# A new plan for the attention steps, and a last layer norm in four pieces, in a one-core decoder block

## The chip, the cores and the metric

The kernel runs on one core of a Trainium2 chip. The metric is device time in microseconds, from the start to the end of one execution. The kernel before has a median of 1132.72 us over 3 runs (1132.64 to 1136.57).

## The reference, cut to what matters

One decoder layer over 256 tokens of width 1024, all in float32. The mixer makes one projection of `x` and runs two attentions on its columns: sliding-window attention with a learned sink per head, and a three-branch sparse attention. The MoE part sends each token to 4 of 32 experts.

```python
h = LayerNorm(alpha * x + Mixer(x))
y = LayerNorm(alpha * h + MoE(h))
# mixer A, per head; mixer B's branches are the same without the sink
s = q @ k.T * scale + bias            # masked to the window
m = max(max(s), sink)
e = exp(s - m)
p = e / (sum(e) + exp(sink - m))
o = p @ v
# MoE, for each expert with its tokens
act = glu * sigmoid(1.702 * glu) * (lin + 1)
out = act @ w_down[e] + b_down[e]
```

## The kernel before, in words

**Three stages.** First comes the mixer. TensorE (PE) runs 32 projection units. A unit is one block of 128 columns: a weight of 8 blocks of 128x128 is multiplied with the 256 tokens, three times, since weights and tokens are split into a high and a low part. So a unit has 24 matmuls and falls into two halves of 12. The halves are numbered h; half h belongs to unit h/2, rounded down. After the units come the branch projections, the output projection, the first layer norm and the router. The second stage is the 32 experts, whose weights (12 MB each) are streamed from memory through ten fixed buffers: a transfer can only start when the buffer's last content has been used up. The third stage is the last layer norm (`finish`) with the output's four transfers.

**How attention is laid between the units.** The 12 head pairs (branch b = 0, 1, 2 and pair r = 0 to 3) each take four steps. S (`scores`, L605): PE makes the scores, VectorE (DVE) adds the bias and takes the row maximum, ScalarE (ACT) takes the exponential and its sum. N (`norm`): DVE inverts the sum, GpSimd (POOL) multiplies four pieces by it. T (`transpose`): six PE transposes into two PSUM tiles, each copied to SBUF as `pT`. V (`pv`): eight matmuls, and the result is taken out of PSUM. So `S10` is the S step of branch 1, pair 0. `PLAN` (L48) says after which half each step is called. `vt` transposes v, `bias1` loads the second bias table into the buffer of the first, `bl` and `bs` load and split the expert biases, `mlp`, `gelu`, `ckv` compute the compressed blocks (tiles `phid`, `phidT`, `pkc`), `ct` and `cp` use them, `sig` takes the sigmoids of the merge gates (tile M).

**What sets the order.** The orders of PE and of the DMA-issuing SyncE queue (SP) are as the program calls them. In the mixer the orders of DVE, ACT and POOL are set by a scheduler when the program is built; after that, every engine works through its own list in order, and an instruction that must wait holds up all that stands behind it. Around the experts and in `finish` all orders are written out.

**Splitting weights.** `prep` calls `split_w` two units ahead: the high part is a rounding copy (on ACT, or on POOL where `POOL_PART` has 'h'), the low part a subtraction (on DVE, or on POOL where it has 'l'). Three buffers `w_j` take turns, so the rounding for unit n must wait until PE has finished unit n-3.

**PSUM tiles that take turns.** The transposes, `pvt`, `phid`, `phidT`, `pct` share two buffers (tag `t`); a step that takes a buffer waits until the tile two places earlier has been copied out. The lines on which the steps rest:

```python
ps_t = ctx.enter_context(tc.tile_pool(name="ps_t", bufs=2, space=PSUM))
ps_s = mx.enter_context(tc.tile_pool(name="ps_s", bufs=3, space=PSUM))
SP.dma_start(T[b], src)             # load_T: both tables in one buffer of tag "T"
```

Of the kernel before, what the change touches and what calls it, by code (L numbers as in the profile page):

```python
# [47 lines left out]
PLAN = {7: 'gates', 8: 'sinks', 9: 'c1', 10: 'gsum S00 S02', 11: 'S01 N00 N01', 12: 'N02', 13: 'T00 S03 N03 bias1 T02', 14: 'vt0 V00 T01', 15: 'V01 blocks', 16: 'V02 T03', 17: 'V03 mlp bl', 19: 'gelu', 20: 'bs', 22: 'bw', 23: 'ckv S10 N10', 24: 'S11 N11 br', 26: 'S12 T10 N12', 27: 'T11 S13 N13', 28: 'vt1 csm', 29: 'T12 V11 S20', 30: 'V10 T13 N20', 31: 'ct V13 vt2', 32: 'S21 V12 T20 cp1 cp0 S22 N22 V20 S23', 33: 'N21 T21 N23', 34: 'cp2 cp3 V21 T22', 35: 'rw V22 T23', 36: 'x V23', 38: 'sel', 39: 'sig'}  # L48
# [11 lines left out]
def tile_block(ctx: ExitStack, tc: tile.TileContext, a, out):  # L60
# [541 lines left out]
    class Pair:  # L602
# [3 lines left out]
        def scores(self):  # L606
# [54 lines left out]

        def transpose(self):
            self.pT = []
            for g in range(2):
# [445 lines left out]
    class Expert:  # L1110
# [3 lines left out]
        def gate_up(self, j):  # L1114
# [91 lines left out]
    def finish():  # L1206
        lo, mid, hi = slice(0, 512), slice(512, SPLIT), slice(SPLIT, D)
        (st0, ag0, rs0), (st1, ag1, rs1) = lns
        g_, b_ = ln2[:, 0], ln2[:, 1]

        def normed(tt, rs):
            o_ = oz[:, tt]
            ACT.activation(o_[:, 512:], yac[tt][1], AF.Identity, bias=rs[:, 0:1], scale=rs[:, 1:2])
            POOL.tensor_tensor(o_[:, hi], o_[:, hi], g_[:, hi], ALU.mult)
            POOL.tensor_tensor(o_[:, hi], o_[:, hi], b_[:, hi], ALU.add)

        def rest(tt):
            o_ = oz[:, tt]
            DVE.tensor_tensor(o_[:, mid], o_[:, mid], g_[:, mid], ALU.mult)
            DVE.tensor_tensor(o_[:, mid], o_[:, mid], b_[:, mid], ALU.add)  # L1220

        for o_ in range(2):
            DVE.bn_stats(st0[:, o_, :], yac[0][o_])
        ln_scale(st0, ag0, rs0)
        for o_ in range(2):
            DVE.bn_stats(st1[:, o_, :], yac[1][o_])
        ln_inv(ag0, rs0)
        normed(0, rs0)
        ln_scale(st1, ag1, rs1)
        ln_mean(oz[:, 0], yac[0][0], g_, lo, ag0)  # L1230
        ln_inv(ag1, rs1)
        normed(1, rs1)
        ln_dev(oz[:, 0], b_, lo, rs0)
        rest(0)
        ln_mean(oz[:, 1], yac[1][0], g_, lo, ag1)
        ln_dev(oz[:, 1], b_, lo, rs1)
# [169 lines left out]
```

## Time and profile before

| | us |
|---|---|
| median of 3 runs | 1132.72 |
| the profiled execution | 1130.43 |
| its span, first to last instruction | 1128.7 |
| mixer, until the first expert's matmuls | 206.7 |
| DVE's first statistics of the last norm | 1114.15 |

PE is busy in 95% of the span, DVE in 26%, ACT in 18%, POOL in 7%. The 16 DMA engines move 438.5 MB, at about 427 GB/s in most slices of the span. A busy PE is not PE at its peak, since the ends of its pipelined matmuls are modelled; the starts of successive instructions tell more. Of a row of the timeline, the first number is the start in us, the second the duration, and the bracket, where there is one, the idle time of that engine before it and what released it.

### The profile page before, as it was taken

The numbers are of one execution on the slowest core, as the hardware profiler recorded it, in microseconds if no ns is written. First come the engines' busy times: TensorE is split into PE (matmuls) and PEld (weight loads), VectorE is DVE, ScalarE is ACT, GpSimd is POOL, SyncE is SP. The second block draws the span as 40 slices with busy tenths as digits, with TensorE's granted clock in tenths as the row PEclk, the third lists the DMA queues.
The fourth block names the chain that finished last, engine by engine and source line by source line (L and its number), as shares of the span: only waits on it lengthen the run. The fifth ranks groups of instructions, "written<-read, shape, count | busy, mean of one in ns | idle before, by whom it ended". The sixth has DMA issues, their size and how long they took to land.

```text
span 1128.7 us, 13459 instructions
## 1 busy us (share of the span) xinstructions
PE 1069.2 (95%) x5660; PEld 509.7 (45%) x5660; DVE 290.0 (26%) x710; ACT 203.8 (18%) x434; POOL 79.4 (7%) x115
## 2 busy tenths in 40 slices
PE   9899999999999999999999999989999998899895
PEld 8787998543434343334343333333333342333322
DVE  4887366311111111111121211111110211020213
ACT  3545344210101110111110101011111110011011
POOL 1545310000000000000000000000000000000001
PEclk9999999999999999999999999999998999999998
DMA  9583777899999999999999999999999999999993
GB/s 335 195 310 137 305 298 299 333 403 418 426 427 426 428 429 427 427 428 426 428 427 427 426 426 427 427 430 427 426 427 427 426 429 427 427 426 427 426 427 123
DMA packets 38288, 438.50 MB, mean 389 GB/s; under 512 B 4032, under 2 KB 6736, under 8 KB 9168
## 3 DMA queue, kind: packets, MB, share of 16 engines
q1 hardware_dynamic: 37888, 436.98, 92.7%
q8 instruction: 46, 0.75, 0.3%
q10 hardware_dynamic: 336, 0.62, 0.2%
q14 instruction: 18, 0.15, 0.0%
HBM read 435.92 MB, written 1.66 MB: 388 GB/s over the span
## 4 chain that ended last, share of the span: by engine, by line


## 5 line engine op out<-in xcount | busy, mean ns | idle before, releaser
L1123 PE MATMUL g<-wg,xeM 128*64 128x512 f32 x1208 | 282.2, 605 | 2.3 <-DMA wg<-in_w_gu_dram 2.2
L1123 PEld LDWEIGHTS g<-wg,xeM 128*64 128x64 f32 x1208 | 83.4, 138 | 157.0 <-issue 140.2
L1145 PE MATMUL pd<-wd,wk 128*64 128x512 f32 x600 | 134.1, 594 | 15.4 <-DMA wd<-in_w_d_dram 15.4
L1123 PE MATMUL g<-wb,xeM 128*64 128x512 f32 x624 | 145.2, 600 | 1.5 <-DMA wb<-in_w_gu_dram 1.5
L1150 DVE COPY y<-pd 64x512 f32<-64x512 f32 x32 | 22.2, 694 | 426.7 <-ACT y L1149 426.7
L1145 PEld LDWEIGHTS pd<-wd,wk 128*64 128x64 f32 x600 | 42.9, 137 | 101.3 <-issue 81.0
L1103 DVE TENSOR_SCALAR gs<-g 128x512 f32<-128x512 f32 x32 | 22.1, 692 | 247.2 <-PE g L1123 247.2
L1123 PEld LDWEIGHTS g<-wb,xeM 128*64 128x64 f32 x624 | 42.9, 138 | 83.2 <-issue 73.9
L1145 PE MATMUL pd<-wb,wk 128*64 128x512 f32 x304 | 69.8, 606 | 7.0 <-DMA wb<-in_w_d_dram 7.0
L1149 ACT COPY y<-pd 64x512 f32<-64x512 f32 x32 | 18.5, 578 | 293.9 <-PE pd L1145 293.9
L247 PE MATMUL pu<-xhl,w_j 128*128 128x256 f32 x240 | 70.1, 292 | 0.0
L1037 POOL TENSOR_SCALAR wk<-const,posm 128x64 f32<-128x64 f32 x30 | 12.8, 446 | 796.4 <-PE pst L1092 792.3
L248 PE MATMUL pu<-xhl,w_j 128*128 128x256 f32 x240 | 67.8, 283 | 0.0
L249 PE MATMUL pu<-xhl,w_j 128*128 128x256 f32 x240 | 67.8, 282 | 0.0
L1078 PEld LDWEIGHTS px<-wk,h_tok 128*128 128x128 f32 x480 | 55.8, 191 | 24.3 <-issue 12.2
L1078 PE MATMUL px<-wk,h_tok 128*128 128x128 f32 x480 | 61.5, 281 | 0.0
L1099 PE MATMUL yac<-y,wk 128*128 128x512 f32 x128 | 59.2, 605 | 0.7 <-ACT y L1149 0.7
L1134 ACT COPY wk<-pa 128x512 f32<-128x512 f32 x32 | 18.8, 586 | 197.1 <-PE pa L1133 185.6
L1123 PE MATMUL g<-wp,xeM 128*64 128x512 f32 x208 | 50.2, 614 | 0.0
L247 PEld LDWEIGHTS pu<-xhl,w_j 128*128 128x128 f32 x240 | 46.0, 192 | 1.9 <-issue 1.0
L1105 ACT ACTIVATE wk<-gs 128x512 f32<-128x512 f32 x31 | 19.5, 630 | 148.7 <-DVE gs L1103 148.6
L248 PEld LDWEIGHTS pu<-xhl,w_j 128*128 128x128 f32 x240 | 45.9, 191 | 0.0
(242 smaller groups left out, 1045.7 us busy)
## 6 DMA issues: line engine op xcount, KB each, us to landing
wg<-in_w_gu_dram SPq DMA_DIRECT2D x72, 2048.0 KB, 38.2
wb<-in_w_gu_dram SPq DMA_DIRECT2D x38, 2048.0 KB, 34.1
wd<-in_w_d_dram SPq DMA_DIRECT2D x36, 2048.0 KB, 39.1
wb<-in_w_d_dram SPq DMA_DIRECT2D x16, 2048.0 KB, 39.1
wp<-in_w_gu_dram SPq DMA_DIRECT2D x12, 2048.0 KB, 37.5
w<-in_w_in_dram SPq DMA_DIRECT2D x14, 1024.0 KB, 8.1
wp<-in_w_d_dram SPq DMA_DIRECT2D x7, 2048.0 KB, 38.4
wg<-in_w_gu_dram SPq DMA_DIRECT2D x7, 1024.0 KB, 10.3
```

The costliest lines, as they stand in the source:

```text
L247: PE.matmul(o_, wh, xh, start=start, stop=False)
L248: PE.matmul(o_, wh, xl, start=False, stop=False)
L249: PE.matmul(o_, wl, xh, start=False, stop=stop)
L1078: PE.matmul(t[:, k * P:(k + 1) * P], h_tok[:, tt, j * P:(j + 1) * P], oh[:, tt].rearrange("p k s -> p (k s)"), start=(tt == 0), stop=(tt = ...
L1099: PE.matmul(yac[tt][o_], st[:, tt * P:(tt + 1) * P], y2[:, o_, :], start=first, stop=last)
L1103: DVE.tensor_scalar_min(g_, gate_, LIMIT)
L1105: ACT.activation(s_, g_, AF.Sigmoid, scale=SW_ALPHA)
L1123: PE.matmul(self.g[b][64 * hf:64 * hf + 64, :], xes[e][:, j, :], w[:, 1024 * b + 512 * hf:1024 * b + 512 * hf + 512], start=False, stop=(j ...
L1134: ACT.copy(aT, t)
L1145: PE.matmul(d[64 * o_:64 * o_ + 64, :], aT[:, P * j + 64 * hf:P * j + 64 * hf + 64], w[j // 2][:, 1024 * (j % 2) + 512 * o_:1024 * (j % 2) ...
L1149: ACT.copy(y2[k, 0, :], d[:CAP])
L1150: DVE.tensor_copy(y2[k, 1, :], d[CAP:])
```

## The change

- `PLAN` is written anew: S, N, T and V of a pair come at set distances, and attention ends after half 38, not 36; `END_H` follows, since the pools are closed there and the experts' buffers `wb` laid in their place.
- `POOL_PART` loses the POOL subtractions ('l') of units 7, 9, 16, 17, 18; units 13 and 16 to 18 get a POOL rounding.
- In branch 0, the sink's exponential gets its own tile `se`, and its call stands ahead of the scores' exponentials.
- Both `pT` copies of a T step are on ACT; one was on DVE.
- At the end, the last expert's transposes are called between the two halves of the expert before it, into a buffer of their own, and its down projection takes another PSUM bank. `finish` handles the output in four quarters: subtract the mean and multiply by the gain on DVE, then for the first token tile scale on ACT and add the offset on POOL, for the second both on DVE.

```diff
-POOL_PART = {6: 'h', 7: 'l', 8: 'h', 9: 'l', 10: 'h', ...
+POOL_PART = {6: 'h', 8: 'h', 10: 'h', 11: 'h', 12: 'h', 13: 'h', ...
-END_H = 36
+END_H = 38
-PLAN = {7: 'gates', 8: 'sinks', 9: 'c1', 10: 'gsum S00 S02', 11: 'S01 N00 N01', 12: 'N02', 13: 'T00 S03 N03 bias1 T02', 14: 'vt0 V00 T01', 15: 'V01 blocks', 16: 'V02 T03', 17: 'V03 mlp bl', 19: 'gelu', 20: 'bs', 22: 'bw', 23: 'ckv S10 N10', 24: 'S11 N11 br', 26: 'S12 T10 N12', 27: 'T11 S13 N13', 28: 'vt1 csm', 29: 'T12 V11 S20', 30: 'V10 T13 N20', 31: 'ct V13 vt2', 32: 'S21 V12 T20 cp1 cp0 S22 N22 V20 S23', 33: 'N21 T21 N23', 34: 'cp2 cp3 V21 T22', 35: 'rw V22 T23', 36: 'x V23', 38: 'sel', 39: 'sig'}
+PLAN = {7: 'gates', 8: 'sinks', 9: 'c1', 10: 'S00', 11: 'N00', 12: 'S01 vt0', 13: 'T00 N01 gsum', 14: 'V00 S02', 15: 'T01 N02 blocks', 16: 'V01 S03 bias1', 17: 'T02 N03 mlp', 18: 'V02 gelu bl', 19: 'T03', 20: 'V03 ckv bs', 22: 'bw S10', 23: 'N10', 24: 'T10 S11 br', 25: 'N11', 26: 'T11 S12', 27: 'S13 N12', 28: 'vt1 csm N13', 29: 'V10 T12', 30: 'V11 S20 T13', 31: 'V12 N20 S21', 32: 'V13 vt2 T20 ct N21', 33: 'cp0 T21 cp1 S22', 34: 'V20 N22 cp2 S23', 35: 'V21 T22 cp3 N23', 36: 'V22 rw', 37: 'T23', 38: 'x V23', 39: 'sel', 40: 'sig'}
             if br == 0:
+                self.se = se = pp.tile([P, 2, 2], F32, tag="se", bufs=2, name=f"se{self.n}")
                 DVE.scalar_tensor_tensor(st, st, -1.0, nsinkx[:, r], ALU.mult, ALU.min)
+                DVE.tensor_tensor(se, st, sinkx[:, r], ALU.add)
+                ACT.activation(se, se, AF.Exp)
...
-            if br == 0:
-                DVE.tensor_tensor(st, st, sinkx[:, r], ALU.add)
-                ACT.activation(st, st, AF.Exp)
...
-                if g:
-                    ACT.copy(pT, t[:, :384])
-                else:
-                    DVE.tensor_copy(pT, t[:, :384])
+                ACT.copy(pT, t[:, :384])
...
+                if between and hf == 0:
+                    between()
...
+        def centred(tt, o_):
+            DVE.scalar_tensor_tensor(oz[:, tt, cols[o_]], yac[tt][o_], lns[tt][1][:, 0:1], g_[:, cols[o_]], ALU.subtract, ALU.mult)
+        def scaled(tt, o_):
+            o2 = oz[:, tt, cols[o_]]
+            ACT.activation(o2, o2, AF.Copy, scale=lns[tt][2][:, 1:2])
+            POOL.tensor_tensor(o2, o2, b_[:, cols[o_]], ALU.add)
+        stats(0, 0)
+        stats(0, 1)
+        ln_scale(*lns[0])
+        centred(0, 0)
+        inverse(0)
+        scaled(0, 0)
+        stats(1, 0)
+        centred(0, 1)
+        scaled(0, 1)
+        stats(1, 1)
+        ln_scale(*lns[1])
+        centred(1, 0)
+        inverse(1)
...
-        ex[E - 2].down()
-        ex[E - 1].transpose()
+        ex[E - 2].down(ex[E - 1].transpose)
```

The plan moves instructions on the engines that the scheduler orders too. In the lists below, `su` is the sum of a pair's exponentials, `st` its negated maximum, `sb` its scores, `z` and `blk` belong to the compressed blocks; in `sb_3_0_570` and the like the 3 is the pair, the 0 the head group.

The first place is DVE where branch 0's pair 0 gets its reciprocal, ahead of its T step. Before:

```order
L652 TENSOR_TENSOR su_0_339<-su_0_339,st_0_338 128x4
L640 TENSOR_TENSOR st_2_359<-st_2_359,sinkx 128x4
L632 SCALAR_TENSOR_TENSOR st_1_394<-st_1_394,nsinkx 128x4
L653 RECIPROCAL su_0_339<-su_0_339 128x4
L652 TENSOR_TENSOR su_2_360<-su_2_360,st_2_359 128x4
L431 TENSOR_SCALAR z_457<-pu_426,pk 64x128 x3
```

And after the change, at the same place:

```order
L450 COPY V<-pvt_406 128x2x128
L632 SCALAR_TENSOR_TENSOR st_1_390<-st_1_390,nsinkx 128x4
L633 TENSOR_TENSOR se_1_398<-st_1_390,sinkx 128x4
L430 TENSOR_SCALAR z_422<-pu_371,pk 64x128 x2
L651 TENSOR_TENSOR su_0_331<-su_0_331,se_0_338 128x4
L430 TENSOR_SCALAR z_422<-pu_371,pk 64x128 x2
L652 RECIPROCAL su_0_331<-su_0_331 128x4
```

The reciprocal of pair 0 has moved behind all four `z` instructions, which read unit 6's result (`pu_371`).

The second place is ACT where the copies of branch 0's transposes stand, around the call of `mlp`. Before:

```order
L637 ACTIVATE sb_3_1_485,su_3_481<-sb_3_1_485,st_3_480 128x128
L221 CAST yhl<-y_0_535 128x256
L641 ACTIVATE st_3_480<-st_3_480 128x4
L671 COPY pT_1_1_552<-t_1_1_548 128x384
L221 CAST yhl<-y_1_570 128x256
L221 CAST yhl<-y_2_600 128x256
L671 COPY pT_3_1_617<-t_3_1_613 128x384
L466 CAST bt<-bt 128x768
```

And after the change:

```order
L639 ACTIVATE sb_3_0_570,su_3_569<-sb_3_0_570,st_3_568 128x256
L639 ACTIVATE sb_3_0_570,su_3_569<-sb_3_0_570,st_3_568 128x128
L639 ACTIVATE sb_3_1_573,su_3_569<-sb_3_1_573,st_3_568 128x256
L634 ACTIVATE se_3_576<-se_3_576 128x4
L639 ACTIVATE sb_3_1_573,su_3_569<-sb_3_1_573,st_3_568 128x128
L416 ACTIVATE kT_598<-pu_542,pk 128x256
L669 COPY pT_2_0_604<-t_2_0_600 128x384
L669 COPY pT_2_1_610<-t_2_1_606 128x384
L465 CAST bt<-bt 128x768 x2
L220 CAST yhl<-y_2_670 128x256
```

The copies of T02 now stand behind the exponentials of S03, and the two casts of the expert biases follow them at once.

The third place is DVE where branch 1's pair 0 gets its reciprocal, ahead of T10. Before:

```order
L653 RECIPROCAL su_0_811<-su_0_811 128x4
L634 TENSOR_SCALAR st_1_857<-st_1_857 128x4
L413 TENSOR_SCALAR qT_707<-pu_838,pk 128x256
L656 TENSOR_TENSOR su_0_811<-su_0_811,g_157 128x4
L225 TENSOR_TENSOR w_j_894<-w_421,w_j_894 128x1024
```

And after the change:

```order
L636 TENSOR_SCALAR st_0_801<-st_0_801 128x4
L412 TENSOR_SCALAR qT_709<-pu_781,pk 128x256
L224 TENSOR_TENSOR w_j_839<-w_366,w_j_839 128x1024
L652 RECIPROCAL su_0_802<-su_0_802 128x4
L655 TENSOR_TENSOR su_0_802<-su_0_802,g_157 128x4
```

The subtraction for unit 14's weights now stands ahead of the reciprocal. On ACT, further on, two of the merge gates' sigmoids are now among the last exponentials: one between T20's and T21's copies, with a table load ahead of it and one behind it, the other behind S23's exponentials and ahead of T22's copies, with one more table load; before, one load stood behind the last exponential.

## Rows read from the trace of the kernel before

**Rows 1.** Busy time of each engine by stretch of the span: PE, weight loads (PEld), DVE, ACT, POOL with their instructions, PE's granted clock (1.00 is 2.4 GHz), busy share of the DMA engines, GB/s. The first row is the mixer with attention, the second the rest of its units, the last two the experts.

```profile
15.40:111.70 96.30, 90.06 (x784) 76.32 (x782) 72.41 (x253) 46.98 (x147) 44.80 (x62) 1.00 0.63 233
111.70:150.70 39.00, 39.00 (x326) 38.97 (x325) 14.07 (x14) 13.94 (x22) 12.47 (x8) 1.00 0.84 329
...
206.70:450.00 243.30, 242.90 (x1170) 92.98 (x1170) 41.95 (x101) 30.09 (x60) 3.42 (x8) 1.00 1.00 419
450.00:1100.00 650.00, 612.48 (x2878) 234.26 (x2876) 107.31 (x233) 76.17 (x153) 8.55 (x20) 0.98 1.01 427
```

**Rows 2.** The same view, for the last stretch before the experts.

```profile
180.00:200.00 20.00, 19.76 (x131) 16.80 (x131) 11.57 (x25) 7.23 (x10) 0.00 (x0) 1.00 0.63 240
```

**Rows 3.** Groups of PE's instructions by line from 22.4 to 111.7 us: count, busy us and mean ns, then idle time ahead of them and who ended it.

```profile
L247 PE MATMUL pu<-xhl,w_j 128*128 128x256 f32 x116 | 34.7, 299 | 0.0
...
L507 PE MATMUL phid<-w_c,blk 128*32 128x128 f32 x64 | 2.0, 274 | 0.0
...
L537 PE MATMUL pkc<-cu,pk 128*64 128x15 f32 x4 | 0.3, 218 | 0.0
```

**Rows 4.** PE's timeline where an S step (L616), a V step (L684) and a T step (L666) follow each other without a wait.

```profile
92.31 0.92 PE L616 MATMUL s<-kT,qT 64*128 64x256 f32 x8
93.17 0.65 PE L684 MATMUL y<-pT,V 128*64 128x256 f32 x4
...
93.97 0.33 PE L666 MATMUL t<-const,sb 128*128 128x128 f32 x1
...
94.77 0.66 PE L587 MATMUL yc<-pcT,vc 32*64 32x256 f32 x8
```

**Rows 5.** The same S step followed through DVE, ACT and POOL (timelines of the three engines): first bias addition, negated maximum, reciprocal; first exponential, and the copy behind the last one; the four multiplications.

```profile
93.38 0.42 DVE L627 CUSTOM_DVE_ANT_0 sb<-s,T 128x256 f32<-128x256 f32 x1 [1.96 <-PE s L616]
...
94.61 0.17 DVE L634 TENSOR_SCALAR st<-st 128x4 f32<-128x4 f32 x1
...
96.77 0.18 DVE L653 RECIPROCAL su<-su 128x4 f32<-128x4 f32 x1 [0.55 <-ACT sb L637]
...
94.87 0.51 ACT L637 ACTIVATE sb<-sb,st 128x256 f32<-128x256 f32 x1 [0.41 <-DVE st L634]
...
96.64 0.46 ACT L671 COPY pT<-t 128x384 f32<-128x384 f32 x1
...
97.32 1.65 POOL L659 TENSOR_SCALAR sb<-sb,su 128x256 f32<-128x256 f32 x4 [3.72 <-DVE su L656]
```

**Rows 6.** Timelines of DVE and POOL: the four `z` of a unit, a pair of additions that branch 1's S steps have besides, a rounding of weights on POOL, a subtraction of weights on DVE.

```profile
46.12 1.46 DVE L431 TENSOR_SCALAR z<-pu,pk 64x128 f32<-64x128 f32 x4 [0.30 <-PE pu L249]
...
67.22 0.25 DVE L646 TENSOR_TENSOR c_s<-s,const 128x15 f32<-128x15 f32 x2
...
47.62 1.05 POOL L219 TENSOR_SCALAR w_j<-w 128x1024 fp32r<-128x1024 f32 x1
...
49.89 1.21 DVE L225 TENSOR_TENSOR w_j<-w,w_j 128x1024 fp32r<-128x1024 f32 x1
```

**Rows 7.** Timelines of POOL and DVE around one of POOL's subtractions.

```profile
39.02 2.38 POOL L223 TENSOR_TENSOR w_j<-w,w_j 128x1024 fp32r<-128x1024 f32 x1
...
39.54 1.89 DVE L652 TENSOR_TENSOR su<-su,st 128x4 f32<-128x4 f32 x1
```

**Rows 8.** ACT's timeline: a cast of the expert biases, and the one table load among the attention steps with the sigmoid behind it.

```profile
51.85 0.83 ACT L466 CAST bt<-bt 128x768 bf16<-128x768 f32 x1
...
104.07 1.28 ACT L725 ACT_TABLE_LOAD   x1
105.36 0.42 ACT L725 ACTIVATE M<-M 128x256 f32<-128x256 f32 x1
```

**Rows 9.** SP's timeline where the second bias table is issued, and the DMA issues of 40 to 60 us with KB each and median us from issue to landing.

```profile
42.01 0.38 SPq L301 DMA_DIRECT2D T<-ud  x1
...
T<-ud SPq DMA_DIRECT2D x1, 1024.0 KB, 5.9
...
bt<-in_b_gu_dram SPq DMA_DIRECT2D x1, 256.0 KB, 8.4
```

**Rows 10.** The end of the experts: PE's timeline (the two halves of the last expert's down projection), SP's issues of the last loads, and of the tiles `wp` and `wb` the time from issue to landing of these loads (the longest of `wp` is its weight load; the two of `wb` are its two pieces).

```profile
1105.26 3.63 PE L1145 MATMUL pd<-wp,wk 128*64 128x512 f32 x16
1108.69 3.63 PE L1145 MATMUL pd<-wb,wk 128*64 128x512 f32 x16
...
1066.59 0.42 SPq L78 DMA_DIRECT2D wp<-in_w_d_dram  x1
1070.57 5.23 SPq L78 DMA_DIRECT2D wb<-in_w_d_dram  x2
...
DMA to landing us min/median/max: 2.1/2.9/38.2
...
DMA to landing us min/median/max: 34.3/35.5/36.8
```

**Rows 11.** The last norm: DVE's first statistics, a 512-column pass over the output, its last pass, and one of POOL's 352-column passes.

```profile
1114.15 0.70 DVE L1223 BATCH_NORM_STATS2 st<-yac 128x6 f32<-128x512 f32 x1 [0.49 <-PE yac L1099]
...
1122.73 0.75 DVE L189 SCALAR_TENSOR_TENSOR wp<-wp,rs,ln 128x512 f32<-128x512 f32 x1
...
1123.75 0.33 DVE L1220 TENSOR_TENSOR wp<-wp,ln 128x160 f32<-128x160 f32 x1
...
1119.63 1.25 POOL L1215 TENSOR_TENSOR wp<-wp,ln 128x352 f32<-128x352 f32 x1
```

More of the change, by code (lines that the diff above doesn't have):

```diff
@@ L36 @@
 NWS, NSB, AHEAD, SIG0 = 3, 6, 2, 20
-POOL_PART = {6: 'h', 7: 'l', 8: 'h', 9: 'l', 10: 'h', 11: 'h', 12: 'h', 14: 'h', 15: 'h', 16: 'l', 17: 'l', 18: 'l', 19: 'h', 20: 'h', 21: 'h', 22: 'h', 23: 'h', 24: 'h', 25: 'h', 27: 'l', 28: 'l', 30: 'l', 38: 'l'}
+POOL_PART = {6: 'h', 8: 'h', 10: 'h', 11: 'h', 12: 'h', 13: 'h', 14: 'h', 15: 'h', 16: 'h', 17: 'h', 18: 'h', 19: 'h', 20: 'h', 21: 'h', 22: 'h', 23: 'h', 24: 'h', 25: 'h', 27: 'l', 28: 'l', 30: 'l', 38: 'l'}
 SIDE_R = "right"
 LOADS, LOADS2 = 6, 11
-END_H = 36
-SPLIT = 672
+END_H = 38
 SPLIT1 = 512
@@ L648, in norm @@
         def norm(self):
-            br, r, st, su = self.br, self.r, self.st, self.su
+            br, r, su = self.br, self.r, self.su
             cols = (slice(S, S + P), slice(0, S))
             if br == 0:
-                DVE.tensor_tensor(su, su, st, ALU.add)
+                DVE.tensor_tensor(su, su, self.se, ALU.add)
             DVE.reciprocal(su, su)
@@ L1125, in gate_up @@
             if j == NJ - 1:
-                swiglu(*self.g, aT if e < E - 1 else y2[:, 1, :])
+                if e == E - 1:
+                    x_ = xe2[0].rearrange("p j s -> p (j s)")
+                    self.aT, s_ = x_[:, :512], x_[:, 512:]
+                else:
+                    self.aT = s_ = aT
+                swiglu(*self.g, s_)
         def transpose(self):
@@ L1133, in transpose, with down @@
                 PE.transpose(t[:, j * P:(j + 1) * P], av[:, j, :], ident)
-            ACT.copy(aT, t)
-        def down(self):
+            ACT.copy(self.aT, t)
+        def down(self, between=None):
             e = self.e
-            d = ps_w.tile([P, 512], F32, tag="w1", name=f"pd{e}")
+            d = ps_w.tile([P, 512], F32, tag="w0" if e == E - 1 else "w1", name=f"pd{e}")
             for o_ in range(2):
@@ L1144, in down @@
                     for o_ in range(2):
-                        PE.matmul(d[64 * o_:64 * o_ + 64, :], aT[:, P * j + 64 * hf:P * j + 64 * hf + 64],
+                        PE.matmul(d[64 * o_:64 * o_ + 64, :], self.aT[:, P * j + 64 * hf:P * j + 64 * hf + 64],
                                   w[j // 2][:, 1024 * (j % 2) + 512 * o_:1024 * (j % 2) + 512 * o_ + 512],
                                   start=False, stop=(hf == 1 and j == 3))
+                if between and hf == 0:
+                    between()
             k = slice(CAP * (e % 2), CAP * (e % 2) + CAP)
@@ L1206, in finish @@
     def finish():
-        lo, mid, hi = slice(0, 512), slice(512, SPLIT), slice(SPLIT, D)
-        (st0, ag0, rs0), (st1, ag1, rs1) = lns
         g_, b_ = ln2[:, 0], ln2[:, 1]
[L1211 to L1220, printed above, removed]
@@ L1222, in finish @@
-        for o_ in range(2):
[L1223 to L1236, printed above, removed]
@@ L1237, in finish, with stats, inverse @@
-        rest(1)
+        cols = slice(0, 512), slice(512, D)
+        def stats(tt, o_):
+            DVE.bn_stats(lns[tt][0][:, o_, :], yac[tt][o_])
+        def centred(tt, o_):
+            DVE.scalar_tensor_tensor(oz[:, tt, cols[o_]], yac[tt][o_], lns[tt][1][:, 0:1], g_[:, cols[o_]], ALU.subtract, ALU.mult)
+        def inverse(tt):
+            DVE.reciprocal(lns[tt][2][:, 1:2], lns[tt][2][:, 0:1])
+        def scaled(tt, o_):
+            o2 = oz[:, tt, cols[o_]]
+            ACT.activation(o2, o2, AF.Copy, scale=lns[tt][2][:, 1:2])
+            POOL.tensor_tensor(o2, o2, b_[:, cols[o_]], ALU.add)
@@ L1238, in finish @@
+        stats(0, 0)
[11 more added lines that the diff above has]
+        inverse(1)
+        for o_ in range(2):
+            if o_:
+                centred(1, 1)
+            ln_dev(oz[:, 1], b_, cols[o_], lns[1][2])
         for tt in range(2):
-            for n, c in enumerate((lo, slice(512, D))):
+            for n, c in enumerate(cols):
```

## The prediction

> **What bounds the kernel now.** I read the stretches of the span first, then PE's groups and timeline in the mixer, then the engines that PE waits for, and the end last. From 206.7 us on, the DMA engines are busy all the time: their share is 1.00 to 450 us and 1.01 to 1100 us [rows 1]. The reader is to see there that PE, though 94 to 100% busy, has no say in this stretch: the remaining weights come at 427 GB/s, and when PE catches up it only waits for them. Before that the share is 0.63, 0.84 and, just ahead of the experts, 0.63 again [rows 1, 2], since the ten buffers are full or not yet free. So the moment at which the mixer ends fixes when the stream is fed steadily, and each microsecond lost or won in the mixer arrives at the end unchanged. Nothing in those rows could absorb a delay: an idle DMA engine there waits for a buffer that PE still holds.
>
> The mixer's attention part is PE's. From 22.4 to 111.7 us, 89.3 us, PE has 29 halves of 12 matmuls, 348 in all (three lines of 116, [rows 3]). Their pace without attention is 39.0 us for 324, 0.120 us each [rows 1], so 41.9 us. Twelve S at 0.86, twelve V at 0.80 and twelve T at 0.80 us [rows 4] are 29.5 us; the ten smaller groups, from the 2.0 us of L507 to the 0.3 us of L537, are 7.7 us busy [rows 3]. That is 79.1 us of work, and about 10.2 us in which PE waited. Some 2.5 us of it may be weight loads at the changes between steps; so 8 to 11.
>
> **The new plan, step by step.** Each of the new plan's waits is worked out from what stands in front of it in the built lists, with the durations of one S step that nothing disturbs. From that S step's start on PE: first bias addition at 1.07, maximum ready at 2.47, exponentials from 2.56 to 4.33, reciprocal at 4.46, the four multiplications from 5.01 to 6.66 us [rows 4, 5]. T can end 0.2 us later. PE covers little of this: a half is 1.44 us (1.53 with its first weight load).
>
> *T10 and T11.* Only two halves lie between S10 and T10, as between S11 and T11: PE comes to T 0.86 + 2 x 1.53 = 3.9 us after S started. Branch 1 has two pairs of additions more, 0.5 us [rows 6], so T can end at 7.3, against 4.7 if nothing were late: 2.6 us. For T10 a second path ends in the same place: the subtraction for unit 14 stands ahead of the reciprocal, needs POOL's rounding, and that needs the end of unit 11, 2.4 us after S10 started: 2.4 + 1.05 + 1.21 [rows 6], the reciprocal and the multiplications with 2.4, gives 7.1. I take 2.5 each, 5.0 (3.6 to 5.2).
>
> *T00.* It follows unit 6's last matmul at once, and DVE has the four `z` of unit 6 (1.46 us, [rows 6]), an addition and the reciprocal (0.35) and starting times ahead: 2.1 us, then the multiplications with 1.65 [rows 5] and 0.2. T00 ends 3.95 us after unit 6 instead of 0.7: 3.3 us (2.5 to 4.5).
>
> *phid and phidT.* `phid` takes the PSUM buffer of T02's first half, and T02's copies stand on ACT behind S03's exponentials and a copy of kT. After S03's end PE is there in 1.53 + 0.7 = 2.25 us; ACT, by the same chain (bias additions to 1.75, exponentials 2.0 with the sink's, two copies of 0.46, [rows 5]), in 4.75: 2.5 us late. Behind that, `phidT` needs a DVE copy that stands behind the bias subtraction, which needs ACT's cast, which needs the load `bl`. SP issues `bl` after the second bias table, which must wait for S03's additions (1.5 us after S03); the table landed 5.9 us after its issue and the biases 8.4 after theirs, with a weight load between them that is now earlier [rows 9]. I take one microsecond behind the table: landing at 8.4, then cast 0.83 [rows 8], subtraction about 1 and copy 0.3: 10.7 against PE's 9.0. 1.7 us (0 to 4). Together 4.2.
>
> *pct* takes the buffer of T20's first half, whose copy stands behind S21's exponentials and a copy of yB on ACT, and DVE has a weight subtraction ahead of S21's additions. PE is there 3.2 us after S21, the copy at 1.1 + 1.4 + 1.9 + 0.9 = 5.3: 2.1 us (1.0 to 2.6).
>
> *V22.* Behind S23's exponentials ACT now has a table load and a sigmoid, 1.28 and 0.42 [rows 8], ahead of T22's copies. PE is at V22 4.9 us after S23; ACT at 1.25 to 2.5 for the additions, 0.4, then 1.8, 1.7 and 0.46: 5.7 to 6.9, and the second copy 0.46 on. 2.2 us (1.0 to 3). The Trainium skill's page ScalarE: Activation LUTs, section What ACT_TABLE_LOAD costs, counts a drain of some 1.4 us to every load, 2.66 us in all. In this trace the next activation starts 1.29 us after the load's start [rows 8], so no drain shows; by the page V22 would be 1.4 us later, and the sum 1.4 us higher.
>
> *V01, V03, V10, T12* have the same form with less: copies behind exponentials, or a V copy behind additions, by 0.6, 0.6, 0.5 and 0.9: 2.6 us (0 to 4). At all other steps PE's distance is over 6.7 us and I price them at nothing.
>
> Sum of the new waits: 5.0 + 3.3 + 4.2 + 2.1 + 2.2 + 2.6 = 19.4 us (10.4 to 25). The old 10.2 go. The attention's work is the same, and the two halves by which it ends later are units that PE runs in any case. The mixer grows by 9.2 us (0 to 15).
>
> **The end.** The last expert's transposes leave PE's path, but not much comes of it. Its weights land at 1066.6 + 38.2 = 1104.8 and 1070.6 + 36.8 = 1107.4, the last piece at 1075.5 + 34.3 = 1109.8, and PE works on them from 1105.26 and 1108.69 [rows 10]: it can be 0.3 us earlier, no more. Of `finish`, DVE took from 1114.15 to 1124.08, 9.9 us [rows 11]. Now it has four statistics of 0.70, four centred passes and two scaled ones of about 0.75 [rows 11], and small ones of some 0.7: 8.0 us, with 0.4 of waiting for ACT's root 8.4. POOL's additions of 512 columns, 1.8 us each by estimate from its 352 [rows 11], lie beside them but for 0.2. So 1.3 to 1.6 us; with the 0.3, 1.9 us saved (1.0 to 2.8), and the last transfer starts that much earlier.
>
> Against the profiled execution: 1130.43 + 9.2 - 1.9 = 1137.7 us. That execution is 2.3 us below the median; on the median's footing the forecast is 1132.72 + 7.3 = 1140.0 us.
>
> **The rivals.** *The plan does what its name says: faster.* One mechanism could carry it: POOL's subtractions. While one ran from 39.02 to 41.40, DVE's 128x4 addition took 1.89 us and ended with it [rows 7], where the reciprocal of the same size takes 0.18 [rows 5]. The change drops five of these, and with them part of each chain. Were the chains so much shorter that only T00's and one other wait stayed (some 4 us), the mixer would lose 6.2 and the end 1.9: 1124.6 us. It decides where S to T falls under the 3.9 us of T10; but the undisturbed step, with no subtraction beside it, already has 6.66. 0.14. The Trainium skill's page SBUF — State Buffer, section Who interferes with whom, says that a DVE instruction with two SBUF inputs waits for the whole of a GpSimd instruction that reads SBUF; the row agrees, and no wait of mine rests on it.
>
> *The waits overlap: no change.* A step that is late gives the engines time for the next, and biases that land early leave only the lower ends: 10.4 us of waits instead of 10.2, and 1.9 saved: 1131.0. The same comes out if the expert stream hides the mixer's delay, against which the idle DMA share of rows 2 speaks. For it: four of the prices are under 1 us each, within what one engine's earlier start can win. 0.26.
>
> *Forecast,* slower by more than the smaller prices: 0.60, with a range of its own from 1135.5 to 1146.
>
> **How the numbers follow.** A measurement of this kernel can tell about 0.5%, 5.7 us, from no change. The range is 1131 to 1146: from the case of no change up to the mixer's higher bounds (13.3 us, with the end's gain). Slower by over 0.5% 0.60, within 0.26, faster 0.14.
>
> **What would show it.** In the profile after: T10 and T11 each with a wait for POOL of about 2 us, T00 with 2 to 3, `phid` waiting for an ACT copy, V22 for ACT behind a table load; V23 ending near 124 us (half 38, which would have ended at 114.6 before); the experts starting near 216 us; DMA at 1.01 afterwards. The forecast is wrong if S to T is below 5 us in the new plan, if the expert stream ends at the old time after a late start, or if the waits at T10 and T11 are under 1 us.

## The result, and the profile after

Six timed executions of the changed kernel have a median of 1149.41 us (1145.77 to 1151.66); the kernel before, beside them, 1134.06 us (1130.93 to 1139.23). The ratio is 1.0126, with a 95% interval of 1.0099 to 1.0153: 15 us slower. Forecast were 1140.0 us and a range of 1131 to 1146: the sign was right, the size was half of what came, and the time lies above the range. The profiled execution took 1151.66 us, with a span of 1149.9. Of all executions on record one stands apart, 3673.5 us of the kernel `later` below; it is left out of that kernel's figures, and why it took so long is not known.

The stages of the changed kernel come first, in the view of [rows 1] with the same columns: the mixer up to the last V step, then seven stretches of 4 us in it, then the experts.

```profile
15.40:134.40 119.00, 100.12 (x805) 83.33 (x803) 69.85 (x248) 51.16 (x158) 38.83 (x62) 0.94 0.52 194
36.00:40.00 4.00, 1.43 (x6) 0.95 (x7) 3.00 (x7) 1.97 (x6) 3.36 (x5) 0.70 0.49 203
40.00:44.00 4.00, 4.00 (x20) 3.77 (x20) 0.92 (x4) 0.72 (x2) 1.36 (x4) 0.50 0.04 12
44.00:48.00 4.00, 4.00 (x35) 3.37 (x34) 2.51 (x13) 1.13 (x4) 0.52 (x1) 0.95 0.00 0
76.00:80.00 4.00, 2.40 (x10) 1.57 (x12) 0.74 (x3) 0.96 (x3) 1.63 (x4) 0.82 0.00 0
80.00:84.00 4.00, 4.00 (x29) 3.63 (x26) 2.09 (x14) 1.49 (x7) 0.87 (x1) 0.75 0.00 0
96.00:100.00 4.00, 2.40 (x13) 1.87 (x14) 2.75 (x9) 2.25 (x8) 4.00 (x7) 0.88 0.95 391
100.00:104.00 4.00, 4.00 (x27) 3.05 (x27) 0.37 (x3) 0.37 (x1) 0.38 (x2) 0.69 0.05 20
...
421.00:1081.00 660.00, 623.08 (x2946) 240.19 (x2944) 109.55 (x240) 76.84 (x154) 9.37 (x22) 0.99 1.01 427
```

The reader is to see two things. The experts' row is that of before: 1.01 and 427 GB/s. And in the mixer the granted clock, 1.00 in the mixer's rows of [rows 1], falls to 0.50 (1.2 of 2.4 GHz) three times. From 40 to 44 us PE is busy all the time, with 20 matmuls in it; from 44 to 48 us, at 0.95, it does 35.

Next, PE's waits in the mixer of the changed kernel, from its timeline, but for three of under 0.3 us, and without the wait of 0.24 us ahead of the router's first matmul, which all traces have and which is counted in none:

```profile
30.45 0.39 PE L248 MATMUL pu<-xhl,w_j 128*128 128x256 f32 x1 [1.38 <-DVE w_j L224]
37.70 0.48 PE L665 MATMUL t<-const,sb 128*128 128x128 f32 x1 [3.16 <-POOL sb L658]
39.47 0.48 PE L665 MATMUL t<-const,sb 128*128 128x128 f32 x1 [0.86 <-POOL sb L658]
56.06 2.05 PE L506 MATMUL phid<-w_c,blk 128*32 128x128 f32 x64 [2.08 <-ACT pT L669]
62.30 0.43 PE L515 MATMUL phidT<-const,hp__651 128*128 128x60 f32 x2 [1.76 <-DVE hp__651 L509]
...
77.48 0.33 PE L665 MATMUL t<-const,sb 128*128 128x128 f32 x1 [2.01 <-POOL sb L658]
86.33 0.33 PE L665 MATMUL t<-const,sb 128*128 128x128 f32 x1 [1.93 <-POOL sb L658]
...
97.48 0.33 PE L665 MATMUL t<-const,sb 128*128 128x128 f32 x1 [1.95 <-POOL sb L658]
...
112.51 0.66 PE L571 MATMUL pct<-const,pc 128*128 128x128 f32 x4 [1.11 <-ACT pT L669]
128.47 0.81 PE L680 MATMUL y<-pT,V 128*64 128x256 f32 x3 [1.36 <-ACT pT L669]
```

With the three left out these 13 brackets sum to 18.3 us. The same reading of the trace of before gives eight brackets and only 5.9 us; its three largest are

```profile
42.97 0.65 PE L684 MATMUL y<-pT,V 128*64 128x256 f32 x4 [1.88 <-DVE V L451]
49.53 0.65 PE L684 MATMUL y<-pT,V 128*64 128x256 f32 x4 [1.03 <-DVE yhl L225]
89.35 0.80 PE L684 MATMUL y<-pT,V 128*64 128x256 f32 x3 [1.10 <-ACT yB L691]
```

The mixer's length is read between two matmuls that both kernels have: PE's first unit matmul on split weights (timeline) and the last of the router's 16 matmuls that read `hT`, called the router's last matmul here (tile `plg`: count, then first and last start). First before, then the changed kernel:

```profile
15.45 0.47 PE L247 MATMUL pu<-xhl,w_j 128*128 128x256 f32 x1
L841 PE MATMUL plg<-hT,const x16: 272/285/298, 189.9 to 196.0; 128*32 128x128 f32 x16
```

```profile
14.76 0.47 PE L246 MATMUL pu<-xhl,w_j 128*128 128x256 f32 x1
L837 PE MATMUL plg<-hT,const x16: 272/285/298, 209.7 to 215.7; 128*32 128x128 f32 x16
```

So 180.6 us became 200.9, 20.4 more. From the router's last matmul to the last norm's first statistics it is 918.2 us before and 920.2 after. From there to the span's end it is 14.5 and 14.0. Of the end, the rows of the changed kernel that answer to [rows 10, 11]: the first of the last down projection's halves, which waits for its load `wp`, the first statistics, and the last scaled pass.

```profile
1126.95 3.65 PE L1146 MATMUL pd<-wp,xeM 128*64 128x512 f32 x16 [1.00 <-DMA wp<-in_w_d_dram]
...
1135.88 0.70 DVE L1214 BATCH_NORM_STATS2 st<-yac 128x6 f32<-128x512 f32 x1 [0.49 <-PE yac L1095]
...
1143.12 0.75 DVE L188 SCALAR_TENSOR_TENSOR wp<-wp,rs,ln 128x512 f32<-128x512 f32 x1
```

From the first statistics to the last large pass's end DVE takes 8.0 us, before 9.9. The two executions lie 21.2 us apart, the medians 15.4: the one of before is among the shortest of that kernel, the one after the longest of its six.

### The profile page after: what moved, and what is told of

It is laid out like the page before. It is cut to its first block, busy times and chain, and to the rows that moved or that the text cites. A ratio compares the mean times of both kernels' runs of the same rounds, so it can differ in the third digit from the quotient of the medians.

```text
span 1149.9 us, 13460 instructions
## 1 busy us (share of the span) xinstructions
PE 1075.6 (94%) x5660; PEld 513.5 (45%) x5660; DVE 284.5 (25%) x699; ACT 207.4 (18%) x444; POOL 70.7 (6%) x112
## 5 line engine op out<-in xcount | busy, mean ns | idle before, releaser
L1146 PE MATMUL pd<-wd,wk 128*64 128x512 f32 x600 | 136.3, 601 | 19.5 <-DMA wd<-in_w_d_dram 19.4
L246 PE MATMUL pu<-xhl,w_j 128*128 128x256 f32 x240 | 71.8, 299 | 0.0
L1146 PE MATMUL pd<-wb,wk 128*64 128x512 f32 x288 | 64.5, 594 | 7.2 <-DMA wb<-in_w_d_dram 7.2
L248 PE MATMUL pu<-xhl,w_j 128*128 128x256 f32 x240 | 69.1, 288 | 1.4 <-DVE w_j L224 1.4
L247 PE MATMUL pu<-xhl,w_j 128*128 128x256 f32 x240 | 69.0, 288 | 0.0
L246 PEld LDWEIGHTS pu<-xhl,w_j 128*128 128x128 f32 x240 | 47.1, 196 | 2.6 <-issue 1.4
L248 PEld LDWEIGHTS pu<-xhl,w_j 128*128 128x128 f32 x240 | 47.1, 196 | 1.6 <-DVE w_j L224 1.6
L247 PEld LDWEIGHTS pu<-xhl,w_j 128*128 128x128 f32 x240 | 47.1, 196 | 0.0
## 6 DMA issues: line engine op xcount, KB each, us to landing
wg<-in_w_gu_dram SPq DMA_DIRECT2D x7, 1024.0 KB, 10.3
```

The source lines that it names most:

```text
L246: PE.matmul(o_, wh, xh, start=start, stop=False)
L247: PE.matmul(o_, wh, xl, start=False, stop=False)
L248: PE.matmul(o_, wl, xh, start=False, stop=stop)
L1146: PE.matmul(d[64 * o_:64 * o_ + 64, :], self.aT[:, P * j + 64 * hf:P * j + 64 * hf + 64], w[j // 2][:, 1024 * (j % 2) + 512 * o_:1024 * (j ...
```

## The experiments

In the table, "mixer" is the length just defined, "waits" the sum of the brackets on PE's rows in it, counted as above, and "low clock" the time at 0.50, summed over stretches of 1 us; these three come from one execution each. Ratios are to the kernel before, timed beside each. Twelve kernels were run.

| kernel | mixer | waits | low clock | ratio (95%) |
|---|---|---|---|---|
| before | 180.6 | 5.9 | 0 | 1 |
| changed | 200.9 | 18.3 | 13.6 | 1.0126 (1.0099 to 1.0153) |
| tail_alone | 182.1 | 7.3 | 0 | 0.9995 (0.9978 to 1.0012) |
| plan_alone | 194.9 | 13.5 | 6.8 | 1.0090 (1.0063 to 1.0118) |
| old_plan | 187.1 | 11.9 | 3.4 | 1.0038 (1.0021 to 1.0055) |
| pool_old | 192.7 | 12.0 | 6.8 | 1.0062 (1.0039 to 1.0086) |
| pool_alone | 182.2 | 5.9 | 3.4 | 0.9990 (0.9976 to 1.0004) |
| fill | 198.4 | 13.5 | 3.4 | 1.0094 (1.0073 to 1.0115) |
| fill2 | 195.6 | 11.9 | 0 | 1.0096 (1.0067 to 1.0124) |
| later | 186.8 | 10.0 | 3.4 | 0.9987 (0.9971 to 1.0003) |
| best2 | 192.1 | 13.5 | 10.3 | 1.0028 (1.0016 to 1.0040) |
| best1 | 184.2 | 6.1 | 6.8 | 0.9987 (0.9971 to 1.0002) |
| best3 | 184.4 | 6.5 | 6.8 | 0.9967 (0.9951 to 0.9984) |
| ladder | 215.6 | 25.9 | 30.7 | 1.0247 (1.0216 to 1.0277) |

How far one execution can be trusted is seen where the attention part is instruction for instruction that of before, in `tail_alone` and, up to its pauses, in `ladder`: its waits come to 5.9 us in before, 7.3 and 6.8 in these two, and its low clock to 0, 0 and 6.8 us.

In all fourteen traces the first statistics come 917.6 to 920.2 us after the router's last matmul, while that matmul moves from 196 to 230 us. That settles one premise of the prediction: the expert stream hides no part of a late mixer.

### Which part of the change

**The end alone**:

```diff
 # kernel before, with the changed code of the last expert and finish
-        ex[E - 2].down()
-        ex[E - 1].transpose()
+        ex[E - 2].down(ex[E - 1].transpose)
...
+        stats(0, 0)
+        stats(0, 1)
+        ln_scale(*lns[0])
...
```

> The kernel before with the edits of the end alone (last expert, finish). Theory A (the loss is the mixer's: its waits, doubled where TensorE's granted clock fell): the mixer ends as before, and the time is 0 to 2 us below before (the trace of the change shows finish 0.5 us shorter, the prediction said 1.9). Rival C (the end costs part of the 15 us: from the router to the first statistics the change took 1.9 us more): 1 to 3 us above before.

1134.42 us against 1135.01, no difference that can be measured. The mixer is not touched, and the end is not where 15 us come from. From the first statistics to the span's end, the four traces with the old `finish` take 14.5 to 14.6 us, the ten with the new one 12.9 to 14.2, 13.6 in the mean. So `finish` gives some 1.0 us.

**The plan alone**:

```diff
 # kernel before
-END_H = 36
+END_H = 38
-PLAN = {... of before}
+PLAN = {... of the change}
```

> The kernel before with the new PLAN and END_H alone; POOL_PART, the sink's exponential and the pT copies as before. Theory A: most of the loss comes with it: 10 to 18 us above before, PE waits of about 2 us at T10 and T11 and of 2 to 3 at T00, and a granted clock under 0.9 behind some of them. Rival B (POOL_PART, the pT copies on ACT and the tile se make the waits): under 5 us above before, T00, T10 and T11 under 1 us each, clock 1.00 in the whole mixer.

1143.55 us, 8.5 above before. T10 waits 2.02, T11 1.45, T00 1.61 us; the largest waits are T03's 2.35 and unit 6's 2.11, which were not expected. The clock falls twice, behind T03's and T10's. The expectation's lower edge was 10, so the plan carries more than half, not all.

**The other edits of attention**, under the old plan:

```diff
 # changed kernel
-POOL_PART, END_H, PLAN = {... of the change}, 38, {... of the change}
+POOL_PART, END_H, PLAN = {... of before}, 36, {... of before}
```

> The changed kernel with PLAN, END_H and POOL_PART of before; the tile se, the pT copies on ACT and the end as changed. Theory A: within 4 us of before (the end gives 0.5 to 2, the copies on ACT may cost some). Rival B: 8 us or more above before.

1138.47 us, 3.5 above before. In its trace 6.9 of the 11.9 us of waits end with a `pT` copy on ACT, V21's 2.92 the largest, where before 0.4 us did: the copies on ACT cost something even in the old plan. The tile `se` was not run apart from them.

**POOL_PART**, taken back in the changed kernel, and put alone into the kernel before:

```diff
 # pool_old: the changed kernel; pool_alone: the kernel before, - and + exchanged
-POOL_PART = {6: 'h', 8: 'h', 10: 'h', 11: 'h', 12: 'h', 13: 'h', ...
+POOL_PART = {6: 'h', 7: 'l', 8: 'h', 9: 'l', 10: 'h', ...
```

> The changed kernel with POOL_PART of before; plan, copies and end as changed. The plan alone lost 12.0 us of the mixer's 19.7 (last router matmul at 208.0, before 196.0, changed 215.7). If POOL_PART carries the other 7.7: that matmul near 209 and some 5 us below the changed kernel. If the pT copies on ACT and the sink's exponential carry them: within 2 us of 215.7.

1141.35 us; the mixer is 8.2 us shorter than in the changed kernel. Unit 6's wait of 1.38 us is gone, T00's 3.16 is 0.45, T12's 1.95 is 0.24; T10, T11 and `phid` wait as long as in the changed kernel or longer (2.02, 2.48, 2.45). Why T00's went is on DVE. First the changed kernel:

```profile
28.03 2.36 DVE L224 TENSOR_TENSOR w_j<-w,w_j 128x1024 fp32r<-128x1024 f32 x2 [3.00 <-ACT w_j L220]
30.31 0.42 DVE L626 CUSTOM_DVE_ANT_0 sb<-s,T 128x256 f32<-128x256 f32 x1
...
35.53 0.73 DVE L430 TENSOR_SCALAR z<-pu,pk 64x128 f32<-64x128 f32 x2
36.29 0.18 DVE L652 RECIPROCAL su<-su 128x4 f32<-128x4 f32 x1
```

And with the old `POOL_PART`:

```profile
26.82 0.42 DVE L626 CUSTOM_DVE_ANT_0 sb<-s,T 128x256 f32<-128x256 f32 x1
...
31.99 0.17 DVE L652 RECIPROCAL su<-su 128x4 f32<-128x4 f32 x1
...
33.55 1.45 DVE L430 TENSOR_SCALAR z<-pu,pk 64x128 f32<-64x128 f32 x4
```

In the changed kernel S00's first addition stands behind two weight subtractions, and the reciprocal lands behind the `z`; with one of them on POOL it is ahead of them.

> The kernel before with the new POOL_PART alone. In the changed kernel, giving POOL back its five subtractions took 8.7 us off the mixer. Theory A, with the five subtractions on DVE as a cost of their own (1.21 us each ahead of bias additions that PE's next steps rest on): 3 to 8 us above before, waits of 1 us or more behind units 6 to 9 and around T12. Rival (they cost only together with the new plan's short distances): within 2 us of before.

1132.17 us, beside 1134.45 of before: not slower. The theory that the five subtractions are a cost of their own on DVE fell. The same edit is worth 8 us in one plan and nothing in the other.

### Whether the low clock is a cost

**Work put into the waits.**

```diff
 # changed kernel, in Pair.transpose
                 t = ps_t.tile([P, 512], F32, tag="t", ...)
+                for i in range(FILL.get((self.n, g), 0)):
+                    PE.matmul(t[:, :S], xh[:, 0, :P], xh[:, 1, :], start=True, stop=True)
```

> The changed kernel, with extra matmuls of 0.12 us whose result is overwritten, put ahead of the transposes that wait: 18 ahead of T00 (2.2 us of a wait of 3.2), 10 each ahead of T10, T11, T12 (1.2 us of 2). The order of all other engines is unchanged. Theory A: these steps start when they did, the granted clock stays at 1.00 there, and some 6 us come back (13.2 us of the mixer ran at half the clock, of them 12.3 us of work): 5 to 7 us below the changed kernel, V23 ending near 128.5 instead of 134.4. Rival D (the lower clock costs nothing, since these steps wait for other engines again): within 1.5 us of the changed kernel or slower.

> As the run with extra matmuls ahead of the waiting transposes, but spread: 20 ahead of T00's first three transposes and 6 ahead of its second three, 8 each ahead of T10, T11, T12; the order of all other engines is that of the changed kernel. The first such run left a fall of the clock at T00 (38 to 43 us, 1.7 us lost). Theory A: no fall at all is left, the last router matmul comes at 209.5 to 211 (215.7 less the 6.2 us that the low clock cost, less what the waits are shorter), and the time is 5 to 7 us below the changed kernel. Rival D: the same 212 or later.

`fill` left one of the falls, at T00, and took 1145.21 us; its mixer is 2.6 us shorter, not the 4.5 by which the cost of the low clock shrank, since some waits grew. In `fill2` no fall is left:

```profile
36.00:40.00 4.00, 3.01 (x23) 2.40 (x22) 2.77 (x7) 1.79 (x4) 4.00 (x7) 1.00 0.73 293
40.00:44.00 4.00, 4.00 (x36) 3.39 (x35) 2.41 (x12) 0.48 (x2) 0.39 (x2) 1.00 0.02 6
76.00:80.00 4.00, 4.00 (x35) 3.79 (x36) 2.09 (x14) 1.93 (x8) 1.06 (x1) 1.00 0.00 0
96.00:100.00 4.00, 4.00 (x38) 3.39 (x37) 1.37 (x9) 1.57 (x4) 0.45 (x2) 1.00 0.04 14
```

Fifty useless matmuls made the mixer 5.4 us shorter, and the median is 5.3 lower, 1144.12 us. The brackets shrank by 6.4 us, to 11.9, but fifty matmuls of 0.12 us fill 6.0 of that, so nearly all of the 5.4 is the clock. Rival D, by which the low clock costs nothing, falls on the traces. The times alone are weaker evidence: the ratio's interval of 1.0067 to 1.0124 overlaps the changed kernel's 1.0099 to 1.0153, and `fill2` has four executions. All six of `fill` (1143.7 to 1145.6 us) lie below all six of the changed kernel (1145.8 to 1151.7), but the two were not timed side by side.

**Pauses in the plain units**, where nothing of attention runs:

```diff
 # kernel before; PLAN has z4 behind half 42, z8 behind 46, z12, z16, z20
+    def pause(n):
+        t = ps_t.tile([P, 512], F32, tag="t", ...)
+        PE.matmul(t[:, :S], xh[:, 0, :P], xh[:, 1, :], start=True, stop=True)
+        for i in range(n):
+            DVE.tensor_copy(scr, scr if i else t[:, :32])
+        t = ps_t.tile([P, 512], F32, tag="t", ...)
+        PE.matmul(t[:32, :P], scr, ident, start=True, stop=True)
```

> The kernel before with five pauses of PE in the plain units after attention (behind halves 42, 46, 50, 54, 58): one matmul, then 4, 8, 12, 16 and 20 dependent DVE copies of 32 columns, then a matmul that needs the last one; by the 0.15 us of DVE's smallest rows some 0.8, 1.4, 2, 2.6 and 3.2 us of idle PE. Theory A (an idle PE makes its clock fall, whatever the work around): behind the pauses of 2 us and more the granted clock drops to 0.50 for some us and a half takes near 3 us instead of 1.45. Rival D (the fall belongs to the attention steps): every half behind a pause at 1.45 us, clock 1.00.

The pauses came out longer (1.73, 2.60, 4.65, 4.62, 5.49 us), since DVE's weight subtractions stood among the copies. The first three, in stretches with PE's clock as the last column but two:

```profile
123.40:125.30 1.90, 0.17 (x3) 0.04 (x2) 1.64 (x5) 0.00 (x0) 0.00 (x0) 1.00 0.00 0
125.30:131.80 6.50, 6.43 (x51) 6.03 (x51) 1.68 (x2) 0.95 (x2) 2.09 (x2) 1.00 1.02 386
131.80:134.30 2.50, 0.00 (x0) 0.01 (x1) 2.13 (x9) 0.00 (x0) 0.00 (x0) 1.00 0.93 397
135.40:138.40 3.00, 3.00 (x16) 3.00 (x16) 0.00 (x0) 1.30 (x2) 0.00 (x0) 0.50 0.20 79
138.80:141.90 3.10, 3.10 (x28) 3.10 (x28) 0.96 (x1) 1.17 (x2) 0.00 (x0) 1.00 0.00 0
142.30:145.20 2.90, 0.00 (x0) 0.00 (x0) 2.76 (x5) 0.00 (x0) 2.26 (x1) 1.00 0.00 0
145.30:152.20 6.90, 5.30 (x24) 4.95 (x25) 1.24 (x7) 1.41 (x2) 0.31 (x1) 0.52 0.98 380
```

Behind 1.73 us of idle PE, nothing. Behind 2.60 us, 3 us of the plain units at 16 matmuls where the next 3.1 us have 28. Behind 4.65 us a low stretch twice as long, begun while PE still waited. So it is the idle PE, not the attention steps.

### Whether the distances make the waits

```diff
 # changed kernel, PLAN
-13: 'T00 N01 gsum', 14: 'V00 S02', 15: 'T01 N02 blocks', 16: 'V01 S03 bias1', 17: 'T02 N03 mlp', 18: 'V02 gelu bl', ...
+13: 'N01 gsum', 14: 'T00 S02', 15: 'V00 T01 N02 blocks', 16: 'V01 S03 bias1', 17: 'T02 N03', 18: 'V02 mlp', ...
-24: 'T10 S11 br', 25: 'N11', 26: 'T11 S12', 27: 'S13 N12', ... 36: 'V22 rw', 37: 'T23'
+24: 'S11 br', 25: 'T10 N11', 26: 'S12', 27: 'T11 N12', ... 36: 'rw', 37: 'V22 T23'
```

> The changed kernel with twelve steps of the plan put one half later (T00, T10, T11, V22, mlp and what follows from them; T12 stays, T13 and V00 too go later). Theory A (the distances of the plan make the waits, and the waits make the clock fall): T00, T10 and T11 wait under 1.7 us each, phid and phidT under 1 us, the granted clock stays at 1.00 or falls once; the last router matmul comes near 203 instead of 215.7, and the time is 8 to 12 us below the changed kernel. Rival B (it is not the distance that counts, but what stands ahead on POOL, DVE and ACT): the waits move with the steps, and less than 4 us come back.

1132.99 us, 16 below the changed kernel and level with before: more than expected. T10 and T11 wait no more, T00 0.89 us, the clock falls once. Three waits were not expected: behind `phid` T03 now waits 1.96 us, V01 1.78 where the changed kernel has none, and V22's wait has passed to `rw`, now ahead of it, with 1.37.

With the old `POOL_PART` on top:

```diff
 # kernel later
-POOL_PART = {6: 'h', 8: 'h', 10: 'h', 11: 'h', 12: 'h', 13: 'h', ...
+POOL_PART = {6: 'h', 7: 'l', 8: 'h', 9: 'l', 10: 'h', ...
```

> The kernel with the steps one half later, and POOL_PART of before as well. Theory A: the waits left behind unit 6 (0.65 and 1.50) and at T00 (0.89) go, V00's 1.78 shrinks, the clock stays at 1.00; the last router matmul comes at 195 to 198 (201.2 with the new POOL_PART), 3 to 5 us below that kernel, so 1129 to 1131: faster than before and than the changed kernel. Otherwise (with the longer distances DVE has room for the subtractions): within 1.5 us of 1133.4.

1137.12 us, 4.1 slower than without it, against the expectation. POOL's timeline of that run, then DVE's:

```profile
27.83 2.35 POOL L222 TENSOR_TENSOR w_j<-w,w_j 128x1024 fp32r<-128x1024 f32 x1
...
42.16 2.39 POOL L222 TENSOR_TENSOR w_j<-w,w_j 128x1024 fp32r<-128x1024 f32 x1
```

```profile
27.89 3.36 DVE L224 TENSOR_TENSOR w_j<-w,w_j 128x1024 fp32r<-128x1024 f32 x1 [3.29 <-POOL w_j L218]
...
43.32 1.25 DVE L632 SCALAR_TENSOR_TENSOR st<-st,nsinkx 128x4 f32<-128x4 f32 x1
```

Started beside POOL's first subtraction, DVE's own takes 3.36 us, where [rows 6] has 1.21, and ends 1.1 us behind it; PE's unit 6 then waits 2.89 us. DVE's 128x4 operation of 1.25 us (0.17 in `later`) ends with POOL's second; V01, which waits for DVE work further down its list, then waits 3.17. The expectation calls this wait V00's, but in the order of the steps V00 stands ahead of it. Without these subtractions the two waits were 0.65 and 1.78, 3.6 us less. That is the hold of [rows 7], the first rival's mechanism: it is real, and in the change its going was outweighed.

### A version that beats both

```diff
 # tail_alone, PLAN; this is best1
-12: 'N02', ... 14: 'vt0 V00 T01', ... 30: 'V10 T13 N20'
+12: 'N02 vt0', ... 14: 'V00 T01', ... 30: 'T13 V10 N20'
```

> The kernel before with the end as changed and three steps of its own plan moved: vt0 from half 14 to 12, V10 behind T13. Theory A, by the waits in the trace of before (V00 1.88 for v's copy, V10 1.10 for ACT's copy): up to 2.5 us of the mixer go, with the end 0 to 1 more: 1131 to 1134, 1 to 3 us below before. Otherwise (the waits move to the next step): within 1 us of before.

1133.20 us: V00 waits no more, but T01 behind it now waits 1.50, and the time cannot be told from before. The 1.10 us that the expectation put down to V10 are V13's in the order of the steps; they are 1.47 now. `pct` waits 1.19, but it does so in the unchanged attention of `tail_alone` too (1.23), so that is not the edit's.

```diff
 # tail_alone; this is best3
-POOL_PART = {... of before}
+POOL_PART = {... of the change}
```

> The kernel before with the new POOL_PART and the new end, and its own plan: the two parts that ran alone at ratios of 0.999 and 0.9995. If their gains add: 1131 to 1133, 1 to 3 us below before, the interval just below 1. If the scheduler lays DVE's instructions less well for the pair of them: 1135 or more.

1130.84 us against 1134.33, as the first branch expected: 0.33% faster than before (0.16 to 0.49%) and 18.6 us below the changed kernel, though the clock falls in its trace too. Neither of its parts could be told from before alone.

## Why the prediction was wrong in its size

**The new waits were right in their paths, and in their sum partly by luck.** Forecast 19.4 us, measured 18.3. T10 and T11 were put at 5.0 and took 3.9, both for POOL; T00 3.3 and 4.0; `phid` and `phidT` 4.2 and 3.8; `pct` 2.1 and 1.1; V22 2.2 and 1.4. Of the small four, 2.6 together, V01 and V03 show none and T12 alone 1.95. Unit 6's wait of 1.38 us, for two weight subtractions that have moved to DVE, was not foreseen. It and T12's, priced at 0.9, make up for about half of what other prices were put too high. (In the price of `phidT` one sum is off: 8.4, 0.83, 1 and 0.3 make 10.5, not 10.7.) The paths are those that were told: at T10 the subtraction ahead of the reciprocal, at V22 the table load behind the exponentials.

```profile
75.26 1.23 DVE L224 TENSOR_TENSOR w_j<-w,w_j 128x1024 fp32r<-128x1024 f32 x1 [0.70 <-POOL w_j L218]
76.40 0.17 DVE L652 RECIPROCAL su<-su 128x4 f32<-128x4 f32 x1
```

```profile
126.34 1.28 ACT L721 ACT_TABLE_LOAD   x1
127.64 0.42 ACT L721 ACTIVATE M<-M 128x256 f32<-128x256 f32 x1
127.96 0.84 ACT L669 COPY pT<-t 128x384 f32<-128x384 f32 x2
```

The activation follows the load's start by 1.30 us, as in [rows 8]; the 2.66 us that the Trainium skill's page ScalarE: Activation LUTs, section What ACT_TABLE_LOAD costs, counts to a load do not show here either.

**First failed step: "The old 10.2 go".** That number was a remainder, 89.3 us less the work at undisturbed pace, and the prediction itself said that some 2.5 us of it might be weight loads at the changes between steps. Such costs are no waits, and the new plan keeps them: PE changes between unit matmuls and other steps 44 times in the trace of before and 52 times in the changed kernel's. The waits proper were in the trace of before as brackets, 5.9 us. Term mis-sized by 4.3 us.

**Second failed step: the sum priced PE's work behind a wait at full pace.** No term stood for the granted clock, because every row of the mixer that was read stands at 1.00 [rows 1]. The changed kernel spends 13.6 us of its mixer at 0.50, and the work in it would have taken 6.2 us less; `fill2` shows that this comes back when PE is kept busy. The Trainium skill's page TensorE: Matmul & The Clock Gate, section HAM oscillation — how this bites in real kernels, tells of matmuls that begin at the low clock each time PE has waited for the DMA. The rows agree in part, with POOL in the place of the DMA: behind T00's, T10's and T12's waits the clock fell, behind T11's 1.93 us and `phid`'s 2.08 it did not.

Together: waits 18.3 - 5.9 = 12.4, clock 6.2, that is 18.6 of the mixer's 20.4 us. The other 1.8 are hardly idle time: gaps too small for a bracket sum to 0.4 us before and 0.7 after. They are matmuls that start further apart at the full clock, as the eight further changes between units and other steps would make them; no run takes these apart. Forecast for the mixer were 9.2, with 15 as the upper bound. With the first term put right the forecast would have been 1144.3 us, with both 1150.5. Of the signs that were named beforehand, V23 ended at 134.4 us, not 124, and the first expert's matmuls started at 226.5, not 216.

**What passed to the end** was as said: the expert stream is fed by the buffers and hides nothing. The 2.0 us by which it differs between the two profiled executions stay open: the changed kernel's is the longest of the fourteen, and the others lie between 917.6 and 919.5. **The end** was put at 1.9 us and gave 1.0, `finish` alone: the last loads bound PE there as forecast.

**The rival "the plan does what its name says"** fell as a forecast, though the POOL hold that it rests on is real. **"The waits overlap"** fell: each wait that was priced over 2 us appeared.

Of the cause this stays open: the kernel before varies from 1130 to 1139 us. In the run `ladder`, whose attention part is instruction for instruction that of before, the clock fell twice there (43 to 47 us and 91 to 94 us), behind waits like those behind which it stayed at 1.00 in before, and V23 came at 113.75 us where before has 110.93. The times on record point the same way: of 88 executions of before that were timed beside four of the groups of runs, the shortest quarter (1130.1 to 1132.5 us) has a mean granted clock of 0.991, the longest (1135.9 to 1138.8) 0.987. That such falls come and go fits the spread, and fits that the medians differ by less than the two profiled executions; but these clocks are means over the whole span, and no run tested it.

## What to carry to other kernels

Count the waits of the kernel before from the brackets on the engine's rows, not as a remainder of its work: the remainder holds costs that stay. Where an edit makes TensorE wait as long as here, look at the granted clock behind the wait and price the work there at half pace, some 1.7 us for a single fall here, and try whether a step put one half later, or even useless matmuls, buys it back. An edit that moves work between engines has no price of its own under a scheduler: the old `POOL_PART` was worth 8 us in one plan, nothing in another, and cost 4 in a third, so measure the pair.

## What was not expected of the hardware

A wait that looks alike need not have the same end: T10's 2.01 us and T12's 1.95 were followed by a fall of the clock, T11's 1.93 between them was not. V00's wait of 1.88 us had no fall behind it in two executions and one in a third, `ladder`, at the same place. Nor does the length of a single wait part the two cases: the clock fell behind T01's 1.50 us in `best1` and S00's 1.55 in `pool_alone`, and stayed at 1.00 behind T10's 2.02 in `pool_old` and unit 6's 2.11 in `plan_alone`. The low stretches behind T10 and T12 were some 3.4 us long, those behind T00 and the pause of 4.65 us about twice that.
